# Job steps of the first group tied to nearby products, wider spacing, a finish of its own for the sample row, and the retention value panels moved

## The chip, the cores and the metric

The kernel runs on one core of one Trainium2 chip. The metric is the device time of one execution in microseconds (us); the time before is the median of three runs, 2477.28 us (2473.57 to 2478.8). The engines are TensorE (PE, matrix products, with PEld for its weight loads), VectorE (DVE), ScalarE (ACT), GpSimd (POOL) and SyncE (SP). Each serves its own queue in order. SP issues most DMAs, ACT and POOL some.

## The reference

One inference step of a layer with two kinds of heads, on 1024 new prompt frames of one stream and 16 new frames of each of 8 running streams. All in fp32; model width 2048, 8 stick-breaking and 8 retention heads of 128.

```
h = rms_norm(x, norm_pre)
q_sb, k_sb, v_sb, gate_sb, q_r, k_r, v_r, gate_r = split(h @ w_in)      # 8 x 1024 columns
q_r, k_r = rope(q_r), rope(k_r) * 128**-0.5

# stick-breaking, per 128 query rows; sample frames see 1024 cached keys and their own
z = q @ k.T * 128**-0.5
log_keep = where(strict, log_sigmoid(-z), 0)
later = reverse_cumsum(log_keep) - log_keep
o_sb = where(strict, exp(log_sigmoid(z) + later), 0) @ v

# retention, chunks of 64: decay inside the chunk, a 128x128 state between chunks
o_r = ((q @ k.T) * intra) @ v + (q @ S) * decay_read
S   = S * gamma**n + (k * decay_write).T @ v

y = concat(head_rms_norm(o_sb) * silu(gate_sb), head_rms_norm(o_r) * silu(gate_r))
x = x + rms_norm(y @ w_out, norm_post)
```

Outputs are the new x of prompt and sample frames, the new key and value rows, and the retention states.

## The kernel before, in words

**Tiles and groups.** The 1024 prompt frames are eight tiles of 128 rows, and the 8 x 16 sample frames a ninth (`SAMPLE`). Two groups go through the input projection one after the other: group 0 has prompt tiles 0 to 3 and the sample tile (640 columns), group 1 has tiles 4 to 7 (512 columns). Every fp32 factor is split into a high and a low part (`split`, L126 to L128: ACT copies the high part, DVE subtracts), and a product is three matmuls.

**Products.** `project` (L219) makes one panel of 128 output columns in four blocks of weights; `products` (L201) issues its matmuls and calls `tick()` after each weight block: 4 x 4 x 3 = 48 ticks a panel. `project_rows` (L229) makes value panels, with the rows as the stationary operand, for two heads at once; it ticks 16 times per row tile. Weights come over SP into four buffers.

**Heads.** A group's loop (L811 to L859) goes over 8 heads. A head projects retention query (column set 4) and key (5), in even heads the retention values of two heads (6, `project_rows`), the retention gate (7), then the stick-breaking query (0) and key (1), in even heads the values of two heads (2, `project_rows`), and the gate (3).

**Jobs.** Everything but the products is written as generators. `Job` (L148) holds one; `tick()` (L153) runs one step of one job that is due; the number that a step yields is the ticks until its next step. `drain` (L166) ticks, without products, until a job has ended. Three jobs run beside the products of group 0:

- `ret_branch` (L755): the keys go to DRAM (`turn_out`, L432, on ACT's queue) and come back with blocks of 32 exchanged (`turn_in`, L438, four DMAs on SP), and DVE transposes them (L765). `retention` (L661) follows, then `sample_retention` (L716) with the running states, then `Out.finish` (L493): head norm, out and back through DRAM, transpose, gain and gate, store. It is created after the gate's projection, and must have ended when the next head's query panel (4) is made.
- `decode` (L566), the sample frames' stick-breaking row: 16 chunks of the key cache over POOL's queue (`load`, L581), each transposed by DVE (L610), products in four batches (`zc`, L601); five loads of the value cache at once on SP (L622), and three more as buffers come free; weights, turned through DRAM; then value products (L648) in one PSUM bank, `pa`, and its evictions (L654 to L657).
- `sb_branch` (L773): four prompt rows (`stick_breaking`, L515): scores, sigmoids, masks on POOL, a scan on DVE, the row out and back through DRAM on POOL's queue, a DVE transpose (L525) and value products (L559). Its `finish` covers all five tiles, and so waits for `decode`. It must have ended before the next head's stick-breaking query is split.

The bank `pa` has one buffer (L414), and all three jobs use it.

**Order.** The order in the code is not yet the order of the queues: the program is given to a planner, which puts each engine's instructions in order by modelled costs and by when their operands are ready. An instruction that is ready early can be placed ahead of its place in the code, and PE's job products are placed where the planner takes their operands to be ready.

**Spacing.** Constants `D_*` at the top (L32 to L50) are ticks; a pair has one number for each group. `D_NAT` is the start of a branch, `D_TO` the ticks from a store to its read-back, `D_TI` from read-back to transpose, `D_TB` from a row's weights to its store.

## Time and profile before

| | |
|---|---|
| median of three runs | 2477.28 us |
| profiled execution | 2463.17 us |
| its span, first to last instruction | 2461.1 us |
| PE busy | 2367.9 us, 96% of the span |
| DVE, ACT, POOL busy | 1250.0, 903.8, 641.9 us |
| mean granted PE clock | 0.988 |
| DMA traffic | 418.65 MB, mean 170 GB/s |

The span begins with the first instruction. Group 0's products start at about 22 us, group 1's at 1166, the output projection's at about 2020. A wait is written as: engine, what waits and its line, what it waited for, then microseconds in total, how often, and the longest. In a timeline line, brackets hold the idle time of the engine before the instruction and what ended it. The granted clock is the share of full speed that PE was given.

### The profile page before, as it was taken

To read this page: it belongs to the slowest core of one execution; us is meant where nothing else is said; L and a number is where in the kernel's file an instruction comes from. 1 tells how busy PE (TensorE), PEld (TensorE's weight loads), DVE (VectorE), ACT (ScalarE), POOL (GpSimd) and SP (SyncE) were. 2 spreads that over 40 slices of the span, in tenths; PEclk is the share of its full clock that TensorE was granted. 3 is DMA by queue.
4 is the path that set the end of the run, shared out by engine and by line. 5 is a ranking of instruction groups with operands and counts; after the bars stand their busy time and mean duration, and the time that the engine had idled before them with its cause. 6 is when DMAs were issued, how large, how long until landed. Compare 5 with 4: busy or idle time off the path is not lost.

```text
span 2461.1 us, 40322 instructions
## 1 busy us (share of the span) xinstructions
PE 2367.9 (96%) x14832; PEld 2099.4 (85%) x14832; DVE 1250.0 (51%) x2362; ACT 903.8 (37%) x1913; POOL 641.9 (26%) x1029
## 2 busy tenths in 40 slices
PE   7999899999999999998799999999999998999998
PEld 7999888989898888988578898889889886878787
DVE  8245454454444454444545544554564555564544
ACT  6323232333233232233334434344344443444333
POOL 3244354443433344333402111120220211000000
PEclk9999999999999999999999999999999998999999
DMA  7769677695948678495955655665564566665553
GB/s 241 165 144 210 143 191 173 173 199 140 212 125 221 149 177 178 130 226 146 209 161 150 153 152 142 144 163 135 153 160 128 152 152 170 224 221 191 184 184 133
DMA packets 673094, 418.65 MB, mean 170 GB/s; under 512 B 223744, under 2 KB 617984, under 8 KB 670464
## 3 DMA queue, kind: packets, MB, share of 16 engines
q1 hardware_dynamic: 523760, 285.99, 45.9%
q0 software_dynamic: 32256, 71.36, 12.5%
q10 hardware_dynamic: 116880, 58.74, 8.6%
q8 instruction: 116, 1.90, 0.3%
q14 instruction: 82, 0.67, 0.1%
HBM read 336.24 MB, written 79.69 MB: 169 GB/s over the span
## 4 chain that ended last, share of the span: by engine, by line
PE 75%; DMA 10%; issue 9%; DVE 4%; POOL 1%; ACT 1%; SPq 0%; ACTq 0%; DVEq 0%; POOLq 0%
PE acc L206 38%; PE accn L252 14%; PE a L890 4%; PE a L891 4%; PE a L889 4%; PE pa L559 2%; DMA vc<-cache_sb_v 2%; PE z L535 2%; DMA wr<-w_in 1%; PE zc L601 1%; DMA ro<-s_rk 1%; DMA kc<-cache_sb_k 1%; DMA s_rk<-rk 1%; PE pa L648 1%; DMA s_be<-be 1%
## 5 line engine op out<-in xcount | busy, mean ns | idle before, releaser
L206 PE MATMUL acc<-ml,wh 128*128 128x256 f32 (+2 forms) x2304 | 677.0, 343 | 0.2 <-DVE ml L128 0.2
L206 PE MATMUL acc<-mh,wh 128*128 128x256 f32 (+2 forms) x2304 | 670.5, 341 | 6.5 <-ACT rv L262 3.8
L206 PE MATMUL acc<-mh,wl 128*128 128x256 f32 (+2 forms) x2304 | 669.9, 341 | 3.7 <-DVE wl L128 3.7
L128 DVE TENSOR_TENSOR wl<-wr,wh 128x512 fp32r<-128x512 f32 (+1 forms) x576 | 394.7, 691 | 503.5 <-ACT wh L127 498.5
L127 ACT ACTIVATE wh<-wr 128x512 fp32r<-128x512 f32 (+1 forms) x576 | 356.6, 625 | 730.4 <-PE acc L206 367.9
L206 PEld LDWEIGHTS acc<-mh,wh 128*128 128x128 f32 x2304 | 425.3, 189 | 51.3 <-issue 14.3
L206 PEld LDWEIGHTS acc<-mh,wl 128*128 128x128 f32 x2304 | 425.1, 189 | 47.6 <-issue 12.2
L206 PEld LDWEIGHTS acc<-ml,wh 128*128 128x128 f32 x2304 | 422.5, 190 | 40.3 <-issue 12.4
L585 POOL DMA_DIRECT2D kc<-cache_sb_k x512 | 331.4, 653 | 367.8 <-DVE kcT L610 167.5
L252 PE MATMUL accn<-whn,mh 128*128 128x256 f32 x1152 | 332.5, 289 | 0.0
L252 PE MATMUL accn<-wln,mh 128*128 128x256 f32 x1152 | 326.9, 284 | 3.8 <-DVE wln L128 3.8
L252 PE MATMUL accn<-whn,ml 128*128 128x256 f32 x1152 | 326.5, 284 | 0.0
L252 PEld LDWEIGHTS accn<-whn,mh 128*128 128x128 f32 x1152 | 221.2, 192 | 12.9 <-issue 10.8
L890 PE MATMUL a<-wl,mh 128*128 128x512 f32 (+1 forms) x576 | 221.2, 384 | 7.7 <-DVE wl L128 7.7
L252 PEld LDWEIGHTS accn<-wln,mh 128*128 128x128 f32 x1152 | 221.3, 192 | 7.0 <-DVE wln L128 5.5
L252 PEld LDWEIGHTS accn<-whn,ml 128*128 128x128 f32 x1152 | 221.0, 192 | 1.7 <-issue 1.7
L891 PE MATMUL a<-wh,ml 128*128 128x512 f32 (+1 forms) x576 | 220.5, 383 | 0.0
L889 PE MATMUL a<-wh,mh 128*128 128x512 f32 (+1 forms) x576 | 219.3, 383 | 1.0 <-DVE sg L279 0.6
L890 PEld LDWEIGHTS a<-wl,mh 128*128 128x128 f32 x576 | 109.3, 190 | 31.3 <-DVE wl L128 10.6
L127 ACT ACTIVATE whn<-wrn 128x512 fp32r<-128x512 f32 x128 | 79.8, 634 | 151.2 <-PE acc L206 39.8
L441 POOL DMA_DIRECT2D be<-s_be x128 | 94.1, 741 | 142.4 <-DMA s_be<-be 124.0
L128 DVE TENSOR_TENSOR wln<-wrn,whn 128x512 fp32r<-128x512 f32 x128 | 86.8, 687 | 83.4 <-ACT whn L127 82.8
(184 smaller groups left out, 2602.4 us busy)
## 6 DMA issues: line engine op xcount, KB each, us to landing
wr<-w_in SPq DMA_DIRECT2D x384, 256.0 KB, 3.8
wr<-w_out SPq DMA_DIRECT2D x184, 256.0 KB, 3.6
wrn<-w_in SPq DMA_DIRECT2D x128, 256.0 KB, 3.1
kc<-cache_sb_k POOLq DMA_DIRECT2D x512, 64.0 KB, 4.3
vc<-cache_sb_v SPq DMA_DIRECT2D x64, 512.0 KB, 8.7
xt<-x_prompt SPq DMA_DIRECT2D x8, 1024.0 KB, 6.1
xr<-x_prompt SPq DMA_DIRECT2D x8, 1024.0 KB, 6.0
out<-out ACTq DMA_DIRECT2D x12, 512.0 KB, 2.9
```

Source lines behind the costliest of these rows:

```text
L127: nc.scalar.activation(hi, src, AF.Copy)
L128: nc.vector.tensor_tensor(lo, src, hi.bitcast(F32), ALU.subtract)
L206: last = nc.tensor.matmul(a[:, :m], lhs[:, j, :], rhs[w][:, j, o : o + m], start=(w == 0 and j == 0 and n == 0), stop=(w == KT // WQ - 1 a ...
L252: nc.tensor.matmul(a, lhs[q][:, jj, ts], rhs[:, j, :], start=(w == 0 and j == 0 and n == 0 and t % 2 == 0), stop=(w == KT // 2 - 1 and j = ...
L441: q.dma_start(raw[32 * i : 32 * i + 32, :].rearrange("p (k a) -> p k a", a=32), s[:, :, 32 * i : 32 * i + 32].rearrange("k (j b) a -> b (k ...
L535: nc.tensor.matmul(z[:, :c], q2[a][:, i * P : (i + 1) * P], k2[b][:, s : s + c], start=(m == 0), stop=(m == 2),)
L559: nc.tensor.matmul(po[:, :P], at[:, j, :], vn[:, j, :], start=(j == 0), stop=(j == t))
L585: nc.gpsimd.dma_start(kc[32 * i : 32 * i + 32, :].rearrange("p (k d) -> p k d", d=32), cache_k[0, 2 * c + j, s * 512 : (s + 1) * 512, h, 3 ...
L601: nc.tensor.matmul(z[r, :], qp[:, j, r], ready[c // 2][:, c % 2, :], start=(j == 0), stop=(j == 1))
L889: nc.tensor.matmul(a[:, :width], hi[q][:, j, ts], wh, start=(k == 0), stop=False)
L890: nc.tensor.matmul(a[:, :width], hi[q][:, j, ts], wl, start=False, stop=False)
L891: nc.tensor.matmul(a[:, :width], lo[q][:, j, ts], wh, start=False, stop=(k == KT - 1))
```

## The change

Six things change; the first four act in group 0 alone.

1. **Tied steps.** `tick` runs a step through the new `tied`. Of each instruction that a group-0 step issues on another engine than PE, it tells the planner to place it after the last product traced before (`anchor`). The dependency orders; it puts no wait on the chip. A job keeps the group in which it was created (`job.phase`).
2. **Spacing.** `D_NAT` 14 to 8, `D_TO` 26 to 32, `D_TI` 12 to 32. A prompt row's store and read-back were 9 ticks apart and are now 9 + 2 + 14 (`D_TA`), with 17 (`D_TB`) from there to the next row's store, in place of 33. Group 1 keeps its numbers.
3. **Value cache.** The first five loads of `decode` become a job of their own, one every 8 ticks (`D_VL`).
4. **Sample row.** `decode` has an output tile and a finish of its own; `sb_branch` finishes four tiles and waits no longer for `decode`. The next head's `decode` is created after the last one has ended.
5. **Value panels** (both groups). The retention value panel of an even head is made at the end of the odd head before it; for head 0 of group 0 it stays after the keys, and for head 0 of group 1 it comes first, with the refill of the moving rows.
6. **Gate** (both groups). The retention job is created before the gate's projection, and waits for the gate only ahead of its finish.

```diff
-D_NAT = (14, 11)
+D_NAT = (8, 11)
+D_VL = 8
-D_TO = (26, 23)
-D_TB = (33, 33)
-D_TI = (12, 13)
+D_TO = (32, 23)
+D_TA = (14, 0)
+D_TB = (17, 33)
+D_TI = (32, 13)
...
+    anchor = [None]
+
+    def tied(job):
+
+        traced = nc.cur_bb.bb.instructions
+        at = len(traced)
+        now, phase[0] = phase[0], job.phase
+        wait = next(job.steps, None)
+        phase[0] = now
+        if job.phase == 0 and anchor[0] is not None:
+            for i in traced[at:]:
+                if i.engine != mybir.EngineType.PE:
+                    tc.add_manual_dep(
+                        i,
+                        anchor[0].ins.name,
+                        mybir.DependencyInfo(mybir.DependencyClass.NoSync, mybir.DependencyReason.SCHED_ONLY),
+                        reason="tied to the products",
+                    )
+        return wait
...
         for job in jobs:
             if job.at <= clock[0]:
-                wait = next(job.steps, None)
+                wait = tied(job)
...
+        def ret_values(g, mov, h, loads=None):
+            pair["r"] = ep.tile([P, 5, 2, P], F32, name="rv", tag="rv")
+            project_rows(g, mov, col(6, h), pair["r"], 0, loads)
+
         def ret_inputs(g, mov, h, acc):
             rq = rope(acc, "rq", *ropes)
             rk = rope(project(g, mov, col(5, h)), "rk", *ropes)
-            if h % 2 == 0:
-                pair["r"] = ep.tile([P, 5, 2, P], F32, name="rv", tag="rv")
-                project_rows(g, mov, col(6, h), pair["r"], 0)
-            rv = pair["r"][:, :, h % 2, :]
-            return rq, rk, rv, gate(project(g, mov, col(7, h)), "rg")
+            return rq, rk, pair["r"][:, :, h % 2, :] if "r" in pair else None
...
             for step in range(len(todo) + lag):
-                if 0 < step <= len(todo):
-                    _, be, turned = rows[step - 1]
-                    turn_in(turned, be, nc.gpsimd)
+                early = D_TA[phase[0]] == 0
+                def read_back():
+                    if 0 < step <= len(todo):
+                        _, be, turned = rows[step - 1]
+                        turn_in(turned, be, nc.gpsimd)
+                if early:
+                    read_back()
...
+                if not early and step <= len(todo):
+                    yield D_TA[phase[0]]
+                    read_back()
                     yield D_TB[phase[0]]
+                if step < len(todo):
+                    if early:
+                        yield D_TB[phase[0]]
...
-        def decode(h, out, qs, rest):
+        def decode(h, qs, rest):
             i = 4
+            out = Out(1, "do")
...
-            values = [load_v(k) for k in range(V_BUFS)]
+            values = []
+            def early():
+                for k in range(V_BUFS):
+                    values.append(load_v(k))
+                    yield D_VL
+            Job(early())
...
-            out.done(i)
+            out.done(0)
+            while "sg" not in rest:
+                yield 3
+            last_row = slice(4 * P, 5 * P)
+            oT = op.tile([P, P], F32, name="doT", tag="doT", bufs=1)
+            Job(out.finish(0, h, rest["sg"][:, last_row], oT, s_y[0][h][:, last_row]))
...
-            while "sg" not in rest or sub is not None and not sub.done:
+            while "sg" not in rest:
                 yield 3
-            yield from out.finish(0, h, rest["sg"], kT, s_y[gi][h])
+            yield from out.finish(0, h, rest["sg"][:, :NB_TOK], kT, s_y[gi][h][:, :NB_TOK])
...
-                    acc = project(g, mov, col(4, h), loads, (0, 1))
-                    loads = None
+                    if h == 0:
+                        ret_values(g, mov, h, loads)
+                        loads = None
+                    acc = project(g, mov, col(4, h))
                     drain(ret_job)
-                    inputs = ret_inputs(g, mov, h, acc)
+                    inputs = *ret_inputs(g, mov, h, acc), {}
                 ret_job = Job(ret_branch(gi, g, h, *inputs), D_NAT[phase[0]])
+                if "rg" not in inputs[-1]:
+                    inputs[-1]["rg"] = gate(project(g, mov, col(7, h)), "rg")
...
-                sub = Job(decode(h, out, qs, rest), D_DEC) if SAMPLE in tiles else None
+                if SAMPLE in tiles:
+                    drain(sub)
+                    sub = Job(decode(h, qs, rest), D_DEC)
...
                 rest["sg"] = gate(project(g, mov, col(3, h), loads, (2, 3)), "sg")
+                if h % 2 and h < H - 1:
+                    ret_values(g, mov, h + 1)
```

More of the change, by code (lines that the diff above doesn't have):

```diff
@@ L150, in __init__ @@
             self.steps, self.at, self.done = steps, clock[0] + after, False
+            self.phase = phase[0]
             jobs.append(self)
@@ L212, in products @@
                     )
+                anchor[0] = last
                 tick()
@@ L227, in tile_hybrid_step, with project_rows @@
     col = lambda i, h: i * H * P + h * P
-    def project_rows(g, mov, col, dst, off):
+    def project_rows(g, mov, col, dst, off, loads=None):
         hi, lo = mov
@@ L240, in project_rows @@
             )
+            for _ in range(WQ if loads and w in (0, 2) else 0):
+                next(loads)
             wh = wp.tile([P, 2, 2 * P], F32R, name="whn", tag="wh")
@@ L249, in project_rows @@
                     for n, (lhs, rhs) in enumerate(((hi, wh), (hi, wl), (lo, wh))):
-                        nc.tensor.matmul(
+                        anchor[0] = nc.tensor.matmul(
                             a,
@@ L405, in tile_hybrid_step @@
             first = ret_inputs(g0, mov, 0, list(zip(acc, g0["pieces"])))
+            ret_values(g0, mov, 0)
+            first = *first[:2], pair["r"][:, :, 0, :], dict(rg=gate(project(g0, mov, col(7, 0)), "rg"))
             drain(job)
@@ L482, in tile_hybrid_step, with __init__ @@
         class Out:
-            def __init__(self, g, tag):
-                nt = len(g["tiles"])
-                self.g, self.nt = g, nt
+            def __init__(self, nt, tag):
+                self.nt = nt
                 self.o = op.tile([P, nt, P], F32, name=tag, tag=tag, bufs=1)
@@ L497, in finish @@
                 )
-                s = turn_out(self.o, f"s_o{b}_{h}_{self.nt}")
+                s = turn_out(self.o, f"s_o{b}_{h}_{self.nt}_{phase[0]}")
                 yield D_TO[phase[0]]
@@ L551, in stick_breaking @@
                     at = kp[:, :n].rearrange("p (k q) -> p k q", q=P)
-                    if step >= len(todo):
+                    if step >= len(todo) and (early or step > len(todo)):
                         yield D_TR[phase[0]]
@@ L652, in decode @@
                     values.append(load_v(k + V_BUFS))
-            od = out.o[:, i, :]
+            od = out.o[:, 0, :]
             nc.vector.tensor_copy(od, po[:, 2 * P : 3 * P])
@@ L753, in sample_retention, with ret_branch @@
             out.done(i)
-        def ret_branch(gi, g, h, rq, rk, rv, rg):
+        def ret_branch(gi, g, h, rq, rk, rv, rest):
             nt = len(g["tiles"])
             rkn = ep.tile([P, 6, P], F32, name="rkn", tag="rkn")
-            out = Out(g, "ro")
+            out = Out(nt, "ro")
             s = turn_out(rk[:, : nt * P].rearrange("p (k t) -> p k t", t=P), f"s_rk{gi}_{h}")
@@ L770, in ret_branch, with sb_branch @@
             yield from retention(gi, g, h, out, rq, rk, rkn, rv)
-            yield from out.finish(1, h, rg, rk, s_y[gi][H + h])
-        def sb_branch(gi, g, h, out, q2, k2, kT, rest, sub):
+            while "rg" not in rest:
+                yield 3
+            yield from out.finish(1, h, rest["rg"], rk, s_y[gi][H + h])
+        def sb_branch(gi, g, h, out, q2, k2, kT, rest):
             tiles, nt = g["tiles"], len(g["tiles"])
@@ L795, in sb_branch @@
                 nc.scalar.dma_start(s_v[h], rest["vn"][:, :4, :])
-            while "sg" not in rest or sub is not None and not sub.done:
+            while "sg" not in rest:
                 yield 3
-            yield from out.finish(0, h, rest["sg"], kT, s_y[gi][h])
+            yield from out.finish(0, h, rest["sg"][:, :NB_TOK], kT, s_y[gi][h][:, :NB_TOK])
         from_h = lambda k: s_h[:, k, :]
         from_y = lambda k: s_y[0][k][:, : 3 * P]
-        ret_job = sb_job = loads = None
+        ret_job = sb_job = sub = loads = None
         for gi, g in enumerate(GROUPS):
@@ L831, in tile_hybrid_step @@
                     nc.scalar.activation(qs, acc[1][0][:, 2 * P : 3 * P], AF.Copy)
-                out = Out(g, "so")
+                out = Out(4, "so")
                 rest = {}
-                sub = Job(decode(h, out, qs, rest), D_DEC) if SAMPLE in tiles else None
+                if SAMPLE in tiles:
+                    drain(sub)
+                    sub = Job(decode(h, qs, rest), D_DEC)
                 acc = project(g, mov, col(1, h))
@@ L846, in tile_hybrid_step @@
                 rest["kT"] = kT
-                sb_job = Job(sb_branch(gi, g, h, out, q2, k2, kT, rest, sub), D_NAT[phase[0]])
+                sb_job = Job(sb_branch(gi, g, h, out, q2, k2, kT, rest), D_NAT[phase[0]])
                 if h % 2 == 0:
```

## The prediction, made before the changed kernel was run

> **What bounds the kernel now.** First the page: its span and its busiest engine.

> ```profile
> span 2461.1 us, 40322 instructions
> PE 2367.9 (96%) x14832; PEld 2099.4 (85%) x14832; DVE 1250.0 (51%) x2362; ACT 903.8 (37%) x1913; POOL 641.9 (26%) x1029
> ```

> TensorE (PE) bounds, and the change takes no product away. It can win only idle PE time and time in which PE runs at a lower clock. So next comes the table of stretches (length, PE busy, PEld, DVE, ACT, POOL, granted clock, DMA share, GB/s): group 0, its border to group 1, group 1, the beginning of the output projection.

> ```profile
> 60.00:1166.00 1106.00, 1071.21 (x7805) 987.33 (x7804) 518.24 (x1045) 344.12 (x763) 434.94 (x724) 0.99 0.75 172
> 1166.00:1258.00 92.00, 78.41 (x457) 58.08 (x456) 46.17 (x79) 31.24 (x61) 26.09 (x45) 0.94 0.84 202
> 1258.00:2007.00 749.00, 748.18 (x4269) 655.32 (x4268) 399.53 (x712) 300.91 (x626) 126.37 (x196) 1.00 0.58 147
> 2007.00:2100.00 93.00, 81.01 (x352) 65.73 (x351) 51.86 (x83) 38.23 (x77) 18.34 (x28) 0.93 0.68 176
> ```

> Group 1 has 0.8 us of idle PE in 749: nothing to win. Group 0 has 1106.00 - 1071.21 = 34.8 us, the border 13.6, together 48.4. The view of waits, PE alone, 60 to 1250 us, names them:

> ```profile
> PE pa L559 <- DVE so L656: 12.2, 4, 7.5
> PE pa L648 <- DMA vc<-cache_sb_v: 9.8, 5, 4.0
> PE rs L668 <- DVE rk L290: 5.1, 1, 5.1
> PE zc L601 <- DVE kcT L610: 3.9, 4, 1.6
> PE acc L206 <- ACT rv L262: 3.8, 2, 2.3
> PE acc L206 <- DVE wl L128: 3.6, 2, 2.1
> PE accn L252 <- DVE wln L128: 3.0, 1, 3.0
> ```

> Few products wait, each for a job step that is late. Each such wait also costs clock. Stretches again (length, PE busy, clock, DMA share, GB/s):

> ```profile
> 263.00:274.00 11.00, 11.00 (x71) 0.84 0.71 133
> 394.00:400.00 6.00, 5.76 (x38) 0.79 1.12 192
> 661.00:664.00 3.00, 1.13 (x10) 1.00 1.15 280
> 664.00:672.00 8.00, 7.62 (x47) 0.79 1.05 200
> 768.00:774.00 6.00, 5.85 (x29) 0.72 1.13 301
> 829.50:836.00 6.50, 6.50 (x37) 0.74 0.53 113
> 1118.00:1126.00 8.00, 7.86 (x40) 0.65 0.33 92
> 1219.00:1229.00 10.00, 10.00 (x71) 0.82 1.07 213
> ```

> Length times the missing share: 1.8, 1.3, 1.7, 1.7, 1.7, 2.8 in group 0 and 1.8 at the border, 12.8 us in all.

> The worst wait shows the mechanism. From the timeline around 1110 us, head 7 (start, length, engine):

> ```profile
> 1092.49 0.38 ACTq L435 DMA_DIRECT2D s_rk<-rk  x1
> 1106.25 0.75 ACT L278 ACTIVATE rg<-acc 128x256 f32<-128x256 f32 x2
> 1104.39 4.13 SPq L441 DMA_DIRECT2D ro<-s_rk  x1
> 1114.26 0.84 DVE L765 STREAM_TRANSPOSE rkn<-ro 128x640 f32<-128x640 f32 x1 [6.48 <-DMA ro<-s_rk]
> 1117.65 0.34 DVE L656 SCALAR_TENSOR_TENSOR so<-pa,dec,so 128x128 f32<-128x128 f32 x1
> 1118.14 1.62 PE L559 MATMUL pa<-vn,kb 128*128 128x128 f32 x6 [7.47 <-DVE so L656]
> ```

> VectorE (DVE) stands 6.48 us before the transpose of the retention keys, because their read-back through DRAM has not landed; queued behind it is the eviction of the one PSUM bank `pa`, and PE needs the bank. The steps do not stand where the program wrote them either: the retention job is created after the gate (L278, 1106.25), plus 14 ticks, yet its first store ran at 1092.49. The planner pulled it forward.

> **The change part by part.** A tick is one weight block's product against the moving rows. A projection has 4 x 4 x 3 = 48, a value panel 8 x 2 x 5 = 80 in group 0, a head pair 12 x 48 + 2 x 80 = 736.

> ```profile
> 486.30:772.70 286.40, 277.97 (x2018) 253.71 (x2017) 136.13 (x277) 88.02 (x197) 117.64 (x197) 0.99 0.78 177
> DMA to landing us min/median/max: 2.1/6.2/13.2
> DMA to landing us min/median/max: 6.3/8.7/15.7
> ```

> So 286.40 / 736 = 0.39 us a tick. The other rows are landings: the retention keys' store and read-back, and the value cache's 512 KB.

> (a) **The bank.** Counting the yields from the start of a sample-row job (`decode`): before, it takes `pa` at tick 255 and frees it at 327, while the prompt rows three and four ask at 256 and 268. Afterwards row four asks at 275, `decode` holds it 281 to 354, and the next head's retention asks at 353. The 12.2 us go. A new handover one tick before the release comes in each of 8 heads: nothing at best, 12.2 / 4 = 3.05 us at worst. I take 0.5, since the evictions are short (0.34 us above) if nothing stands before them: +4.0. Net -8.2.

> (b) **Value cache loads.** Five in a lump become one every 8 ticks (3.1 us), the last three stay. The longer spacing keeps their users from being bunched: D_TI from 12 ticks (4.7 us, under the 6.2 us median) to 32 (12.4 us), D_TO from 26 to 32. Of 9.8 us I take two thirds, -6.5 (none to all).

> (c) **Weights behind the lump.** SyncE's queue (SP) is served in order, and the weights stand behind the lump:

> ```profile
> 756.58 7.86 SPq L616 DMA_DIRECT2D vc<-cache_sb_v  x4
> 764.53 4.85 SPq L192 DMA_DIRECT2D wr<-w_in  x2
> SPq L192 <- DVE wl L128: 197.6, 77, 6.9
> ```

> The products that then wait, or wait for evictions behind late weights, are 3.8 + 3.6 = 7.4 us. Two thirds: -4.9. The third row is SP waiting for free weight buffers, 197.6 us in group 0: weights are usually ahead, which also covers four more read-backs per head for the sample row.

> (d) **Border.** Its 13.6 us idle are partly jobs run out with no products between them. An odd head offers the retention job 4 x 48 = 192 ticks, and it needs 14+26+12+9+72+45+26+12 = 216. With the value panel at the odd head's end it has 5 x 48 + 80 = 320 for 8+32+32+9+72+45+32+32 = 262. The refill of the moving rows stays, so half: -6.8 (none to all).

> (e) **Tying.** The dependency only orders queues; nothing waits for it on the chip. But it takes away head starts, above all of the key cache:

> ```profile
> 526.88 1.30 DVE L610 STREAM_TRANSPOSE kcT<-kc 128x512 f32<-128x512 f32 x2 [1.51 <-PE pa L648]
> 557.49 0.28 ACT L831 ACTIVATE qs<-acc 128x128 f32<-128x128 f32 x1 [0.88 <-DVE ql L128]
> DVE kcT L610 <- DMA kc<-cache_sb_k: 49.2, 16, 5.2
> L585 POOL DMA_DIRECT2D kc<-cache_sb_k x497 | 321.7, 653 | 367.2 <-DVE kcT L610 167.5 <-DVE wl L128 72.9 <-DMA kc<-cache_sb_k 23.0
> ```

> Head 3's job follows L831 at 557.49, its first key transposes ran at 526.88. Tied, a chunk is asked for one step, 12 ticks or 4.7 us, ahead of its transpose, and four issues at 653 ns take 2.6 of them. Behind GpSimd's (POOL) loads stand the read-backs of the prompt rows, which DVE transposes for PE; behind a waiting key transpose stand DVE's weight splits. Products of the keys come in 8 x 4 = 32 batches; they wait 3.9 us now, the longest 1.6. Bounds: -3.9, and 32 x 1.6 - 3.9 = +47. I take +4, a doubling: the 12 ticks between two chunks stay as they were, and only four batches wait now.

> (f) **Clock.** (a) to (e) remove 22.4 of 48.4 us; of 12.8 us of clock the same share, -5.9. [...]

> (g) **At nothing.** The sample row's own finish adds to each head:

> ```profile
> L136 ACT ACT_TABLE_LOAD x14 | 18.0, 1283 | 0.2
> L137 DVE RECIPROCAL or<-or 128x5 f32<-128x5 f32 x14 | 2.6, 188 | 8.8 <-ACT or L136 8.7
> L505 DVE SCALAR_TENSOR_TENSOR rg<-rk,gains,rg 128x640 f32<-128x640 f32 x7 | 6.2, 885 | 0.1
> ```

> At most two table loads, 2 x 1283 ns on ScalarE (ACT), and six small and three larger DVE operations, at most 6 x 0.19 + 3 x 0.89 = 3.8 us. Over 8 heads that is 21 us beside 762 idle of ACT and 30 beside 588 idle of DVE. The weights' lead covers it; uncovered, 51 us. Later read-backs on POOL (14 ticks) cost nothing while prompt rows keep their distance: store to transpose stays about 51 ticks (53 before). Group 1's moved panel: 0 (-0.8; +4 at 1 us per pair, my estimate by its clean row). Output projection: its 12.0 idle stays.

> Sum: -8.2 - 6.5 - 4.9 - 6.8 + 4.0 - 5.9 = -28.3 us. The profiled execution took 2463.2 us (span 2461.1) and would take 2435. The runs shown have a median of 2477.3, 14.1 above that execution, so I add it back: **2449**.

> **The rivals.** Slower: **the head's end becomes a meeting place.** From tick 290 on, SP has the last three value loads (290, 299, 308), then the retention read-back (312) and the finish's (316), eight DMAs. At 344 and 348 DVE has a transpose for each, and behind these the bank's eviction, needed at 353: the queue of 1114 us again, in every head. For it speaks the 13.2 us maximum landing against 32 ticks; against it the 6.2 median. The sum without (a)'s +4.0 is -32.3, so it decides from 4.0 us a head. At 5.4, a little over the mean wait with its clock (3.05 + 1.8), 43 - 32 = +11: 2488.

> **Keys lag.** If the last three of four batches in each head wait 0.97 us (3.9 / 4), that is 24 x 0.97 - 3.9 = +19 in place of +4: 2464. For it: 49.2 us of DVE waits already; against it: PE's 3.9.

> **The order does not decide.** Engines run ahead until a semaphore stops them, tied or not; the same landings come late and the stalls change only their names: 2475. The long distances in (b) speak against it.

> **Most stalls vanish.** All 48.4 + 12.8 would be 61; half of what I left in place gives -45: 2432. Group 1's clean row speaks for it; group 0's DMA share of 0.75 against 0.58, against it.

> **How the numbers follow.** Forecast 0.40, keys lag 0.17, most vanish 0.15: faster 0.72. Order does not decide: 0.11, within 0.2% (5 us, about what a measurement here can tell). Meeting place: slower, 0.17. The range reaches into both far cases: 2424 (-53, near the 61) to 2487 (the meeting place's price). The forecast's own range is 2438 to 2460.

> **What would show it.** Right: group 0's idle PE at 15 to 22 us; no wait of `pa` L559 for `so` L656; retention's first store after its place; the value loads single in SP's queue; fewer stretches under full clock. Wrong: `pa` of the retention (L686) waiting for the sample row's eviction (the meeting place), `zc` over 15 us (keys lag), as much idle as before under other names, or new idle in group 1.

## The result: slower by 4.3%, and the profile after

The changed kernel takes 2582.16 us (median of four runs, 2575.27 to 2590.15) against 2477.32 us before: a ratio of 1.0427, 95% interval 1.0395 to 1.0459. The forecast was 2449, its range ended at 2487. The prediction is wrong in sign and in size.

The profiled execution after took 2582.37 us, close to its median; the one before lies 14 us under its own, so the 119.4 us between the two spans below are 105 us by the medians. The page after, its span and engines:

```profile
span 2580.5 us, 40427 instructions
PE 2443.7 (95%) x14832; PEld 2125.0 (82%) x14832; DVE 1260.7 (49%) x2434; ACT 891.7 (35%) x1915; POOL 653.2 (25%) x1029
```

PE issues the same 14832 matmuls as before and is *busy* 75.8 us longer (2443.7 - 2367.9); idle, the span less that, went from 93.2 to 136.8. A prediction that looks only at idle time misses the larger part.

Stretches after: group 0, the border up to head 1 of group 1, the rest of group 1 (length, PE busy, PEld, DVE, ACT, POOL, clock, DMA share, GB/s):

```profile
60.00:1249.50 1189.50, 1131.48 (x7836) 1004.69 (x7835) 528.81 (x1126) 349.12 (x781) 426.07 (x710) 0.98 0.70 161
1249.50:1428.70 179.20, 153.59 (x842) 122.78 (x842) 85.27 (x164) 57.51 (x122) 42.17 (x72) 0.90 0.71 170
1428.70:2140.30 711.60, 703.18 (x3924) 610.34 (x3923) 380.75 (x663) 273.52 (x580) 133.81 (x187) 1.00 0.58 144
```

The last two of these of the kernel before:

```profile
1166.00:1322.10 156.10, 142.51 (x863) 114.51 (x862) 79.20 (x145) 56.38 (x118) 31.71 (x55) 0.97 0.73 181
1322.10:2023.00 700.90, 699.93 (x3936) 611.90 (x3935) 376.34 (x663) 285.47 (x590) 123.54 (x192) 1.00 0.58 147
```

Group 0 grew by 83.5 us (1106.00 before), the border by 23.1, group 1 by 10.7 (which the experiments put down to the moved panels, not the tie). The view of groups, shapes apart, says what PE is busy with. After, and then before (busy in us, mean ns, idle ahead of it):

```profile
L640 PE MATMUL zc<-kcT,qp 128*32 128x512 f32 x256 | 97.3, 608 | 9.3 <-DVE kcT L649 5.1 <-DVE kb L481 3.9
```

```profile
L601 PE MATMUL zc<-kcT,qp 128*32 128x512 f32 x256 | 48.6, 605 | 5.0 <-DVE kcT L610 3.9 <-DVE kb L454 1.0
```

The same 256 matmuls of the same duration cover 97.3 us in place of 48.6. They are the sample row's products with the cached keys. Each uses 32 of the array's columns, and a batch has eight: four column strips, two matmuls in each. The timeline shows how they lie (start, length, engine and line, matmuls in the run). Before, head 3, whose six runs have 8, 8, 8, 2, 4 and 2 matmuls:

```profile
607.25 1.06 PE L601 MATMUL zc<-kcT,qp 128*32 128x512 f32 x8
...
616.59 1.04 PE L601 MATMUL zc<-kcT,qp 128*32 128x512 f32 x2
...
618.06 1.05 PE L601 MATMUL zc<-kcT,qp 128*32 128x512 f32 x4
...
623.53 1.04 PE L601 MATMUL zc<-kcT,qp 128*32 128x512 f32 x2 [1.58 <-DVE kcT L610]
```

After, head 4, whose ten runs have 8, 6, 2, 4 and then six times 2:

```profile
773.64 1.06 PE L640 MATMUL zc<-kcT,qp 128*32 128x512 f32 x8
...
838.46 1.04 PE L640 MATMUL zc<-kcT,qp 128*32 128x512 f32 x2
...
845.86 1.04 PE L640 MATMUL zc<-kcT,qp 128*32 128x512 f32 x2
...
853.31 1.04 PE L640 MATMUL zc<-kcT,qp 128*32 128x512 f32 x2
```

Eight in four strips take 1.06 us, two in one strip 1.04: in these rows the strips of one run overlap in time (the 256 matmuls of 605 ns before make 155 us, and PE was busy with them for 48.6), and a strip among other products took as long as four together. Counted over the whole trace there were 46 runs before and 93 after.

**Why they are split.** The key transposes stand later in DVE's queue. In the groups of DVE after, and then before (busy, mean ns, idle ahead and what ended it):

```profile
L649 DVE STREAM_TRANSPOSE kcT<-kc 128x512 f32<-128x512 f32 x128 | 89.8, 704 | 0.1
```

```profile
L610 DVE STREAM_TRANSPOSE kcT<-kc 128x512 f32<-128x512 f32 x128 | 89.2, 703 | 60.8 <-DMA kc<-cache_sb_k 53.4 <-PE pa L648 7.4
```

Before, DVE stood 53.4 us for key data: the transposes stood so early in its queue that they waited for the DMA. After, they wait for nothing; the data lies there (a median of 15.8 us, from the landings and starts of all 128), and the queue comes to them late. The views of the tile, one head each, with the first and the last start in us; before, head 3, whose query `qs` was ready at 557.49:

```profile
L610 DVE STREAM_TRANSPOSE kcT<-kc x16: 668/705/712, 526.9 to 622.8; 128x512 f32<-128x512 f32 x16
```

After, head 4, whose query and the next one are in ScalarE's timeline:

```profile
746.15 0.28 ACT L889 ACTIVATE qs<-acc 128x128 f32<-128x128 f32 x1 [0.55 <-DVE ql L130]
...
897.70 0.28 ACT L889 ACTIVATE qs<-acc 128x128 f32<-128x128 f32 x1 [0.55 <-DVE ql L130]
```

and its transposes:

```profile
L649 DVE STREAM_TRANSPOSE kcT<-kc x16: 700/706/711, 754.8 to 864.7; 128x512 f32<-128x512 f32 x16
```

The 16 transposes take about as long (96 us, then 110), but they began 31 us ahead of the query and now begin 9 us behind it. So the keys are done 118 us after the query, where it was 65 (over all eight heads: 118 to 132, before 54 to 88). In head 4 each of the last six runs holds one strip and starts 0.8 to 2.8 us after the start of a chunk's transpose, ahead of the next one's (838.46, 845.86 and 853.31 are 7.4 us apart). That the strips of a batch become ready together while chunks are turned ahead of the query, and that the planner otherwise puts each among the products as it comes, is my reading of the two heads; the batch at 607.25 in head 3, whole though its chunks were turned 12 to 34 us behind the query, fits it badly.

**The other two parts.** The rest of the sample row moves back with the keys, to the head's end. PE's waits after, 60 to 1430 us:

```profile
PE pa L694 <- DMA vc<-cache_sb_v: 27.6, 14, 5.0
PE pa L597 <- DVE kb L557: 18.0, 7, 3.5
PE pa L737 <- DVE sc L721: 8.7, 6, 1.7
PE zc L640 <- DVE kcT L649: 5.1, 7, 0.8
...
PE pa L737 <- DVE do L702: 3.7, 2, 2.4
```

The value products of head 4 still run at 909 us, after the next head's query at 897.70. The tile's view of the value cache, 746 to 1000 us (two heads' 64 products each):

```profile
L694 PE MATMUL pa<-vc,kp x128: 379/379/403, 746.1 to 909.5; 128*32 128x256 f32 x128
```

In all seven heads that have a next one, the row's last value product starts 11 to 21 us after the next head's query, where it stood 13 to 26 us ahead of it before. PE's waits for the value loads grew from 9.8 us to 27.6. Then the clock: one minus its mean, times the span, is 0.021 x 2580.5 = 54.2 us, and 0.012 x 2461.1 = 29.5 before. The strips' 48.7, idle time's 43.6 and the clock's 24.7 make 117.0 of the 119.4 us. This is an estimate: some 5 us of the clock's growth fall on idle time and stand in two of the terms.

### The profile page after: what moved, and what is told of

Its sections match the earlier page's. It is cut to its first block, busy times and chain, and to the rows that moved or that the text cites. A ratio compares the mean times of both kernels' runs of the same rounds, so it can differ in the third digit from the quotient of the medians.

```text
span 2580.5 us, 40427 instructions
## 1 busy us (share of the span) xinstructions
PE 2443.7 (95%) x14832; PEld 2125.0 (82%) x14832; DVE 1260.7 (49%) x2434; ACT 891.7 (35%) x1915; POOL 653.2 (25%) x1029
## 3 DMA queue, kind: packets, MB, share of 16 engines
q1 hardware_dynamic: 524272, 285.99, 43.6%
## 4 chain that ended last, share of the span: by engine, by line
PE 61%; issue 17%; DMA 10%; DVE 5%; SPq 3%; POOL 2%; ACT 2%; DVEq 0%; POOLq 0%; ACTq 0%
PE acc L228 28%; PE accn L277 15%; PE a L952 3%; PE a L953 3%; PE a L951 3%; PE zc L640 2%; DMA mr<-s_y 2%; DMA kb<-s_be 2%; PE pa L597 2%; SPq L468 2%; PE z L567 1%; DMA wr<-w_in 1%; DMA ro<-s_rk 1%; DMA mr<-s_h 1%; DMA s_be<-be 1%
## 5 line engine op out<-in xcount | busy, mean ns | idle before, releaser
L277 PEld LDWEIGHTS accn<-whn,mh 128*128 128x128 f32 x1152 | 222.1, 194 | 27.6 <-issue 20.1
L129 ACT ACTIVATE whn<-wrn 128x512 fp32r<-128x512 f32 x128 | 78.9, 636 | 175.5 <-PE accn L277 75.1
L130 DVE TENSOR_TENSOR wln<-wrn,whn 128x512 fp32r<-128x512 f32 x128 | 88.7, 702 | 97.9 <-ACT whn L129 89.5
L951 PEld LDWEIGHTS a<-wh,mh 128*128 128x128 f32 x576 | 109.7, 190 | 23.2 <-DVE sg L304 1.8
```

The lines of the kernel that those rows point to most:

```text
L129: nc.scalar.activation(hi, src, AF.Copy)
L130: nc.vector.tensor_tensor(lo, src, hi.bitcast(F32), ALU.subtract)
L277: anchor[0] = nc.tensor.matmul(a, lhs[q][:, jj, ts], rhs[:, j, :], start=(w == 0 and j == 0 and n == 0 and t % 2 == 0), stop=(w == KT // 2 ...
L951: nc.tensor.matmul(a[:, :width], hi[q][:, j, ts], wh, start=(k == 0), stop=False)
```

## The experiments

Each ratio is to the kernel before, run on the same chip. The rows come from several chips, on which the kernel before took 2469 to 2482 us, so rows are compared by their ratios. "Idle" is the span less PE's busy time; `zc` is the busy time of the key products' group, as above, and "runs" counts its runs in PE's queue. "Keys end" says when a head's last key transpose starts, in us after the head's query, over the eight heads.

| kernel | median us | ratio, 95% interval | PE busy | idle | `zc` | runs | keys end |
|---|---|---|---|---|---|---|---|
| before | 2477.32 | 1 | 2367.9 | 93.2 | 48.6 | 46 | 54 to 88 |
| after | 2582.16 | 1.0427 (1.0395 to 1.0459) | 2443.7 | 136.8 | 97.3 | 93 | 118 to 132 |
| after_notie | 2451.71 | 0.9881 (0.9852 to 0.9909) | 2371.3 | 79.1 | 44.8 | 42 | 71 to 88 |
| before_tie | 2553.17 | 1.0298 (1.0266 to 1.0329) | 2447.5 | 104.8 | 119.1 | 119 | 118 to 132 |
| after_pack | 2539.53 | 1.0237 (1.0202 to 1.0271) | 2373.9 | 157.0 | 34.1 | 32 | 111 to 126 |
| before_pack | 2498.16 | 1.0078 (1.0052 to 1.0105) | 2366.7 | 129.7 | 35.7 | 32 | 54 to 85 |
| after_keysfree | 2456.58 | 0.9940 (0.9920 to 0.9961) | 2367.5 | 88.7 | 48.6 | 46 | 73 to 95 |
| after_loadsfree | 2501.23 | 1.0117 (1.0089 to 1.0145) | 2399.8 | 98.0 | 79.0 | 72 | 94 to 108 |
| after_keysonly | 2624.68 | 1.0611 (1.0579 to 1.0643) | 2475.5 | 150.1 | 118.7 | 111 | 123 to 138 |
| after_ahead | 2574.09 | 1.0404 (1.0370 to 1.0437) | 2441.3 | 127.7 | 102.2 | 98 | 112 to 129 |
| after_spload | 2623.33 | 1.0594 (1.0568 to 1.0620) | 2457.2 | 159.6 | 98.5 | 88 | 89 to 101 |
| after_actload | 2588.15 | 1.0452 (1.0423 to 1.0481) | 2463.6 | 124.2 | 116.1 | 107 | 82 to 103 |
| after_zc6 | 2595.57 | 1.0482 (1.0454 to 1.0510) | 2473.6 | 122.8 | 131.4 | 126 | 119 to 127 |
| notie_oldspacing | 2473.02 | 1.0027 (1.0004 to 1.0050) | 2369.3 | 108.5 | 40.4 | 37 | 63 to 88 |
| notie_oldpanels | 2466.40 | 0.9997 (0.9978 to 1.0015) | 2373.9 | 89.8 | 49.9 | 46 | 57 to 88 |
| notie_onefinish | 2443.63 | 0.9899 (0.9863 to 0.9934) | 2370.5 | 75.1 | 48.7 | 46 | 71 to 88 |
| notie_pack | 2451.47 | 0.9927 (0.9903 to 0.9950) | 2365.8 | 84.3 | 35.0 | 32 | 73 to 87 |
| notie_g1old | 2432.36 | 0.9823 (0.9797 to 0.9849) | 2362.8 | 67.6 | 47.5 | 44 | 71 to 88 |
| notie_g1panels | 2436.26 | 0.9844 (0.9816 to 0.9873) | 2363.8 | 66.2 | 46.6 | 44 | 71 to 88 |
| notie_g1old_onefinish | 2422.70 | 0.9789 (0.9763 to 0.9814) | 2363.0 | 56.8 | 52.0 | 49 | 71 to 88 |

### The tie alone, taken away and put in

Everything of the change but the tie:

```diff
-        if job.phase == 0 and anchor[0] is not None:
+        if False:
```

> The changed kernel without the dependency on the product (all its other parts stay). Tie theory: the tie is what splits the zc batches (42 runs here, 93 with it: 50 us) and what slows the key phase of the sample row (120 us from its start, 65 before); both go, 2470 to 2500. Rival (the moved panels, spacing or the sample row's own finish are the cost): stays above 2550.

The kernel before with the tie and nothing else (`tied` and `anchor` as in the change):

```diff
-                wait = next(job.steps, None)
+                wait = tied(job)
```

> The kernel before with the dependency alone. Tie theory: 113 runs of zc in place of 46, that is +66 us, and the key phase slows as well: 2540 to 2600. Rival: the tie costs only together with the other parts: within 15 us of 2477.

The tie alone makes the kernel before 3.0% slower; without it the other five parts make it 1.2% faster, more than was expected. After less after_notie is 130.1 us of span: `zc` 52.5, idle 57.7, clock 22.3 (54.2 against 0.013 x 2450.4 = 31.9), 132.5 in sum. The stretches of after_notie, as above:

```profile
60.00:1131.60 1071.60, 1063.19 (x7827) 980.66 (x7826) 529.97 (x1117) 364.13 (x789) 439.41 (x725) 1.00 0.82 178
1131.60:1294.70 163.10, 145.53 (x841) 119.58 (x841) 79.06 (x146) 57.63 (x118) 35.08 (x58) 0.93 0.73 176
1294.70:2008.20 713.50, 704.96 (x3924) 611.26 (x3923) 380.87 (x664) 273.69 (x580) 132.68 (x187) 1.00 0.58 144
```

Group 0 has 8.4 us of idle PE left (34.8 before) and the full clock. Two of its waits, over the whole run, against 27.6 and 3.7 with the tie:

```profile
PE pa L694 <- DMA vc<-cache_sb_v: 2.9, 1, 2.9
PE pa L737 <- DVE do L702: 1.8, 1, 1.8
```

### The strips

The four strips of a batch are told to stand behind the newest, so that they stand together, in three kernels:

```diff
-                    for c in range(4):
+                    newest = None
+                    for c in (3, 2, 1, 0):
...
+                        with tc.issue_after(newest.ins) if newest is not None else nullcontext():
+                            strip = nc.tensor.matmul(
+                                z[r, :], qp[:, j, r], ready[c // 2][:, c % 2, :], start=(j == 0), stop=(j == 1)
+                            )
```

> The changed kernel, where the four key products of a batch (zc, strips of 32 columns of the array) are put in the queue next to each other, behind the one with the newest chunk. Strip theory: a run of zc products costs 0.98 us however many strips stand in it; the changed kernel has 93 runs, this one 32, so about 60 us less: 2522, with PE busy on zc at 32 us in place of 97. Waiting theory (the time went into PE waiting for late operands, and the strips are filler in those waits): less than 15 us change, 2567 or more. If the strips' new place makes a batch wait for its last chunk, zc waits rise above 20 us and part of the gain is lost.

> The kernel before with the four strips of a batch next to each other: 32 runs of zc in place of 46. Strip theory: 14 x 0.98 = 14 us less, 2463. Waiting theory: no change, or slower where a batch waits for its last chunk (PE waits for kcT 3.9 us before).

> The changed kernel without the tie, with the four strips of a key batch next to each other: 32 runs in place of 42, 10 us less. With the key phase done on time a batch should not wait for its newest chunk (the kernel before with the same edit was 17 us slower, with 11 us more waiting for kcT), so 0.984 to 0.988. If it waits as there: 0.992 or more.

In after_pack all 32 batches are whole. PE is busy 69.8 us less, so the split does cost; but by the ratios the run is only 47 us shorter. PE does not wait longer for the keys themselves; what follows them comes later still, as its waits show (27.6 and 18.0 us in the changed kernel):

```profile
PE pa L698 <- DMA vc<-cache_sb_v: 45.3, 19, 5.4
PE pa L597 <- DVE kb L557: 27.8, 12, 6.7
...
PE zc L642 <- DVE kcT L653: 3.7, 9, 0.8
```

In the kernel before, where a gain of some 14 us was expected, packing lost 0.8%. PE now waits for whole batches (14.9 us, 3.9 before), and its wait for the sample row's eviction doubles (12.2 before):

```profile
PE pa L559 <- DVE so L660: 24.1, 5, 7.1
PE zc L603 <- DVE kcT L614: 14.9, 5, 8.2
```

Without the tie it changes nothing that the intervals separate (0.9927 against 0.9881); the gain that was expected of it did not come. So the split goes with late keys (93 runs in the changed kernel, 46 before); it is dear where keys are late, and forbidding it gives part of its price back as idle time (157.0 us in after_pack, 136.8 in the changed kernel).

### Which part of the tie

The key loads and transposes are left out of the tie, then the loads alone, and then only they are tied (`keys` holds their names):

```diff
-                if i.engine != mybir.EngineType.PE:
+                if i.engine != mybir.EngineType.PE and i.name not in keys:
...
-                    nc.gpsimd.dma_start(
+                    asked = nc.gpsimd.dma_start(
...
+                    keys.add(asked.ins.name)
...
-                    nc.vector.transpose(ready[-1][:, m % 2, :], loaded.pop(0))
+                    turned_key = nc.vector.transpose(ready[-1][:, m % 2, :], loaded.pop(0))
+                    keys.add(turned_key.ins.name)
```

> The changed kernel, with the key cache's loads and their transposes left out of the tie; everything else stays tied. Key theory (the whole cost of the tie is that the sample row's key phase falls behind its place: 120 us from its start in place of 73): the key phase is back at 75 us or less, 46 runs of zc, 2450 to 2475. Rival (all tied steps cost a share): 2500 or more, with the key phase short and PE still idle 110 us or more.

> The same with only the loads left out; the transposes stay tied. If the missing head start of the loads is the cause, the key phase is near 75 us and the time within 20 us of the kernel with both left out; 72 runs of zc then still cost 26 x 0.98 = 25 us more than its 46, so 2475 to 2500. If the tied transposes are the cause, the key phase stays above 100 us and the time above 2530.

> The changed kernel with the tie on the key cache's loads and transposes alone. Key theory: most of the tie's 130 us are here, 2550 or more, 110 runs of zc. Rival: under 2510.

With the keys free, 4.9 of the 5.5 points between after and after_notie are gone; tying everything else costs the other 0.6. Tying the keys alone is worse than tying all; why, no run shows. With free loads and tied transposes the result lies between the two cases that were expected: 1.8 of the 4.9 points remain, and the keys end 94 to 108 us after the query. DVE's row shows that what remains is the transposes' place, since no data is waited for:

```profile
L651 DVE STREAM_TRANSPOSE kcT<-kc 128x512 f32<-128x512 f32 x128 | 89.8, 703 | 0.0
```

### What stretches the keys' 16 steps

Asked for earlier, four chunks ahead with five buffers; a yield of 6 ticks for 12 between the steps; and the loads on another queue than POOL's, SP's or ACT's:

```diff
-KC_AHEAD = 2
+KC_AHEAD = 4
...
-                kc = ip.tile([P, 512], F32, name="kc", tag="kc", bufs=3)
+                kc = ip.tile([P, 512], F32, name="kc", tag="kc", bufs=5)
```

> The changed kernel, all tied, with the key cache asked for four chunks ahead instead of two (five buffers instead of three). If the distance of one step between a tied load and its transpose is what stretches the key phase, it ends before 90 us from its start and the time falls below 2530. If the planner's place for tied steps stretches it whatever the distance (the order shows 97 runs of zc, as many as in the changed kernel), the phase stays above 105 us and the time within 25 us of 2582.

```diff
-D_ZC = 12
+D_ZC = 6
```

> The changed kernel with a key step every 6 ticks in place of 12. If the yields set the pace of the key phase, it falls well under 100 us from 120. If a queue sets it (the transposes stand at 284 to 332 ticks as in the changed kernel), it stays above 110 us; 124 runs of zc cost 31 x 0.98 = 30 us more than 93, and the time is 2590 to 2630.

```diff
-                    nc.gpsimd.dma_start(
+                    nc.sync.dma_start(
```

> The changed kernel, all tied, with the key cache asked for on SyncE's queue instead of GpSimd's. In DVE's queue the last key transpose of a head then stands 176 to 200 ticks after the head's start (counted by the weight splits ahead of it), as its yields have it, in place of 296. GpSimd theory (tied loads queue up behind the prompt rows' steps on GpSimd, and the planner puts the transposes where it takes them to land): key phase 65 to 85 us in place of 120, and without its waits the time is 2500 to 2540, with 83 runs of zc still costing 40 us more than 42. Rival (the phase is stretched by the tied transposes themselves): 100 us or more, 2560 or more.

```diff
-                    nc.gpsimd.dma_start(
+                    nc.scalar.dma_start(
```

> The same on ScalarE's queue: transposes stand at 164 to 188 ticks, 107 runs of zc. GpSimd theory: key phase 65 to 85 us; runs cost 65 x 0.98 = 64 us more than the 42 without the tie, so 2510 to 2550. Rival: 100 us or more, 2560 or more. Issues on ScalarE can delay the weight splits; then ACT's idle time for them shows it.

None helps. Earlier loads and shorter yields leave the end of the keys where it was, 112 to 129 us after the query, so neither the distance from a load to its transpose nor the yields set it. Off POOL's queue the keys end 82 to 103 us after it, between the two cases that were expected: POOL's queue accounts for some 30 us. But `zc` stays split, and SP, expected to win 40 to 80 us, loses 41. The key loads now stand in the queue of the weights, and PE waits for the high parts that ACT makes of the weights (0.5 and 0.9 us in the changed kernel):

```profile
PE acc L228 <- ACT wh L129: 57.5, 10, 9.1
PE accn L277 <- ACT whn L129: 19.3, 8, 8.0
```

With ACT's queue the same wait is 25.4 us. What else stretches the 16 steps, no run shows.

### What the untied change lives on

Without the tie, one other part is undone at a time: the spacing, the panels with the gate, the finish.

```diff
-D_NAT = (8, 11)
+D_NAT = (14, 11)
...
-D_TO = (32, 23)
-D_TA = (14, 0)
-D_TB = (17, 33)
-D_TI = (32, 13)
+D_TO = (26, 23)
+D_TA = (0, 0)
+D_TB = (33, 33)
+D_TI = (12, 13)
```

> The changed kernel without the tie and with group 0's spacing as before (D_NAT 14, D_TO 26, D_TI 12, read-back right after the store). The kernel without the tie is at 0.988 of the kernel before. If the spacing carries the gain, this one falls back to 0.996 or more; if the panels or the sample row's finish carry it, it stays below 0.991.

```diff
...
+            if h % 2 == 0:
+                ret_values(g, mov, h)
+            return rq, rk, pair["r"][:, :, h % 2, :], dict(rg=gate(project(g, mov, col(7, h)), "rg"))
...
-                if h % 2 and h < H - 1:
-                    ret_values(g, mov, h + 1)
```

> The changed kernel without the tie and with value panels and gate where they were. Then odd heads offer the retention job 192 ticks for 262 needed, and it is run out without products, 70 ticks in each of four heads. If the panels carry the gain: 1.000 or more. If not: within 0.004 of 0.988.

```diff
...
-            out = Out(1, "do")
...
-            while "sg" not in rest:
+            while "sg" not in rest or sub is not None and not sub.done:
...
-                out = Out(4, "so")
+                out = Out(nt, "so")
```

> The changed kernel without the tie, with one finish for all five tiles that waits for the sample row. With the wide spacing the sample row and the finish need 354 + 64 = 418 ticks of 368, so the last 50 are run out without products. If the own finish carries the gain: 0.996 or more. If not: within 0.004 of 0.988.

The gain needs both the spacing and the panels: undone, either takes it all. (The panels were undone beside the wide spacing only, where an odd head without them offers the retention job 192 of its 262 ticks; with the old spacing they were not tried.) With the old spacing PE waits for the sample row again, in group 0:

```profile
PE pa L687 <- DVE kp L681: 19.5, 6, 5.9
PE pa L597 <- DVE do L702: 11.9, 6, 3.8
```

The second is the old wait for the bank (12.2 us before) with the sample row's new tile name. The finish of its own is not needed. With the old panels, group 0 takes 1095.3 us in place of 1071.6, with 26.1 us of idle PE in place of 8.4; but group 1 gives something back. Its length was 698 to 701 us in the four kernels that have the old panel order and 710 to 714 in the thirteen that have the new one. In notie_oldpanels:

```profile
1325.30:2026.10 700.80, 699.83 (x3936) 611.86 (x3935) 375.75 (x663) 285.80 (x589) 123.70 (x191) 1.00 0.58 147
```

### The panels moved in group 0 alone

The tie is off here too.

```diff
...
+                    *inputs, _ = ret_inputs(g, mov, h, acc)
+                    if gi == 1 and h % 2 == 0:
+                        ret_values(g, mov, h)
+                    inputs = *inputs, pair["r"][:, :, h % 2, :], {}
+                    if gi == 1:
+                        inputs[-1]["rg"] = gate(project(g, mov, col(7, h)), "rg")
...
-                if h % 2 and h < H - 1:
+                if gi == 0 and h % 2 and h < H - 1:
```

> No tying; the moved panels and the later gate only in group 0, group 1 in the order of before. In the runs so far group 1 (first product of its head 1 to its last product) took 698 to 701 us with the old order (four kernels) and 710 to 714 with the moved one (thirteen), while group 0 took 1095 with old panels and 1072 with moved ones. If these two are separate costs, group 1 takes 701 here, group 0 1072, and the time is 12 us under the version without tying: ratio to before 0.983. Rival: the border pays it back (its 163 us grow, as in the kernel with old panels, to 170), and the ratio is 0.986 to 0.988.

The same without the last two added lines, so that only the panels are back:

> As the one before, but with group 1's retention jobs created before the gate's projection (only the panels are back in the old place). If the panels' place costs group 1 its 12 us, group 1 takes 701 here too; if the gate's place does, 713; if both share it, between.

> As the first of the three, and the sample row's finish together with the prompt rows' as before. The finish of its own moved nothing beyond the interval so far (0.9899 against 0.9881), so this stands within 0.3% of the first: ratio 0.981 to 0.986. Rival: with the shorter border of that kernel (152 us against 163) the gain adds up to 0.979.

Group 1 takes 700.9 us again, and 699.1 with only the panels back: the panels' place costs it the 12 us, not the gate's. Group 0 keeps its 1073.6 and 1075.0. The third kernel, without the tie, with the panels moved in group 0 alone and the common finish, is the fastest of all, 2.1% under before; its rival's 0.979 came, not the expected 0.981 to 0.986. Its stretches:

```profile
60.00:1139.20 1079.20, 1072.86 (x7855) 984.12 (x7854) 523.31 (x1061) 331.33 (x756) 439.51 (x729) 1.00 0.80 177
1139.20:1279.80 140.60, 137.12 (x826) 110.84 (x825) 74.09 (x131) 54.69 (x112) 32.28 (x54) 1.00 0.79 195
1279.80:1980.10 700.30, 699.21 (x3933) 611.30 (x3933) 376.89 (x663) 284.28 (x587) 120.11 (x187) 1.00 0.58 146
```

Its gain over notie_g1old lies in the border, 140.6 us against 159.3, at the full clock (group 0 is 5.6 us longer); the intervals of the two ratios (0.9763 to 0.9814, 0.9797 to 0.9849) overlap a little. Why the border is shorter with the common finish is not shown.

## Why the prediction was wrong, point by point

**Step (e), the tying, failed**: +4.0 us was taken, bounded at +47, and it costs 130. The mechanism was named (the key cache loses its head start, shown with the transposes at 526.88 ahead of the query at 557.49), but two things in its price were wrong.

First, the price was a *wait*: 32 batches times the longest wait of 1.6 us. I took a batch as one thing that runs or waits. It is four strips, which came to stand apart (93 runs in place of 46), and the cost of that appears in PE's busy time (97.3 us in place of 48.6), at full "use" of the engine. The waits of `zc` for the keys came to 5.1 us (3.9 before), all its idle time to 9.3; the mark that I had set for lagging keys, "`zc` over 15 us", would have denied what happened. A batch split in three, at 616.59 to 623.53, was in the trace that I had.

Second, I took the 12 ticks between two chunks as the pace of the keys. The pace did change little: in the heads shown the 16 steps took 96 us with the head start and 110 after. But both are more than the 16 x 12 x 0.39 = 75 that the yields write. The head start had hidden that; without it the end moves by 53 us, the row's later steps pass the next head's query, and from there come the waits for values and evictions, 57.7 us of idle, and the clock behind them.

**Keys lag**, the rival with 0.17, is thus nearest to what came, but its price was a wait too (24 batches of 0.97 us), and the tie's 130 us are seven times its +19. **Slower through the meeting place** did not come: PE's wait of L737 for the sample row's eviction is 3.7 us in two places, where that rival had 43. **The order does not decide** is refuted by before_tie: the tie alone, which only orders, cost 3.0%.

**(a) to (d) and (f) came near in sum without the tie, and that was luck.** Forecast -28.3 - 4.0 = -32.3; after_notie has a ratio of 0.9881, -29.5 us on 2477.3. But by the stretches of the two profiled executions, group 0 is 34.4 us shorter, more than was forecast for it, and the border and group 1, which were to win 6.8 and nothing, are 7.0 and 12.6 us longer. (These two executions differ by 10.7 us only, since the one before lies under its median.)

- (a), (b), (c): right where they act. In group 0 the prompt rows' wait for the sample row's eviction (12.2 us) is gone, the value loads' wait fell from 9.8 to 2.9 us (-6.9, forecast -6.5), of the 7.4 us of waits behind late weights 1.1 are left, and idle fell by 26.4 us where these three stood for 19.6. notie_oldspacing shows that the spacing carries (a): the bank's wait came back with 11.9 us.
- (d), the border, -6.8: wrong. In after_notie it took 163.1 us, 7.0 more than before, at a clock of 0.93; the common finish makes it shorter by 11.4 us in one pair of profiled executions (151.7 against 163.1) and by 18.7 in the other (140.6 against 159.3). What the panels save beside the wide spacing lies in group 0.
- (f), the clock, followed the waits, but won nothing in sum: without the tie group 0 has 1.00 and the border 0.93 (0.97 before), and the whole run has 0.987 against 0.988. Nor did each wait cost clock, as the prediction has it: in the trace before, from 60 to 1250 us, PE stood idle for 1 us or more 20 times, and the clock fell 7 times.
- (g), at nothing: the finish of its own costs nothing measurable in after_notie (0.9881 against 0.9899 with the common one). The moved panels in group 1, taken at 0 with +4 as the bound, cost 12 us: in after_notie PE is idle 8.5 us there and busy 5.0 longer, against 0.97 us idle before. I judged group 1 by its clean row as a stretch with room, when it had no idle time to cover a new order.

## What to carry to other kernels

Where small matmuls run in column strips, count their *runs* in PE's queue and not only their number or their waits: here a run took 1.04 us with one strip and 1.06 with four, and late keys split batches (93 runs in place of 46) with hardly any new wait (5.1 us in place of 3.9). The order of the queues that was written by hand took away a head start that the planner had found (31 us ahead of the query, then 9 behind it), so before tying a job, look in the trace for what it does ahead of its place in the code, and leave that part free. A move that wins in a stretch with idle time should be made in that stretch alone: the same panels won 24 us in group 0, beside the wide spacing, and lost 12 in group 1.

## What the runs showed of the hardware that was not expected

A run of key products took 1.04 us with two matmuls in one strip and 1.06 with eight in four, as shown above.

The clock fell after a shorter stall than the 1.9 us (3.00 - 1.13) of idle time in the prediction's row at 661, and stayed after a longer one. The timeline after, PE at 266 and 912 us, with the idle time ahead in brackets, and then the stretches around the two (length, PE busy, clock, DMA share, GB/s):

```profile
266.77 0.94 PE L597 MATMUL pa<-vn,kb 128*128 128x128 f32 x6 [2.92 <-DVE kb L557]
...
912.78 0.46 PE L737 MATMUL pa<-rv,sc 128*128 128x128 f32 x2 [1.66 <-DVE sc L721]
```

```profile
261.96:265.37 3.41, 1.89 (x14) 1.00 1.01 206
265.37:268.79 3.42, 2.02 (x15) 1.00 0.87 211
268.79:272.20 3.41, 3.41 (x26) 1.00 0.67 122
910.50:913.91 3.41, 1.66 (x12) 1.00 1.14 215
913.91:917.33 3.42, 3.42 (x16) 0.50 1.20 222
917.33:920.74 3.41, 3.41 (x26) 1.00 1.14 284
```
